# Token rows in float32 for the experts' gathers, and two more slots in the weights' ring

## The chip, the cores and the metric

One core of one Trainium2 chip. The metric is the device time of one execution in microseconds (us). The kernel before took 3013.36 us (median of three runs, 3009.52 to 3018.86). A difference of about 0.3%, 9 us, is what a measurement of this kernel can tell from none.

## The reference

Two blocks of two layers each work on 512 tokens of width 1024. The change lies in the second block, in its mixture of experts, which both layers of that block have:

```python
def ec_moe(h, w_router, w_gate, w_up, w_down):      # h: (1, 512, 1024), 16 experts
    cap = max(1, EC_FACTOR * n // N_EXPERTS)        # 64 tokens for each expert
    aff = softmax(einsum('bnd,de->bne', h, w_router))
    gate, idx = top_k(swapaxes(aff, 1, 2), cap)
    xs = h[idx]                                     # every expert's own 64 tokens
    a = silu(einsum('becd,edf->becf', xs, w_gate)) * einsum('becd,edf->becf', xs, w_up)
    out = einsum('becf,efd->becd', a, w_down) * gate[..., None]
    return zeros.at[idx].add(out)
...
# second_block: layer 0 = even mixer, ec_moe; layer 1 = pool mixer (w_in_odd, w_pool_grp), ec_moe; then a norm
```

Each of w_gate, w_up and w_down is 16 x 1024 x 1024 float32 in either layer: 192 MB a layer.

## The kernel before, in words

The stages follow one another: the first block, the even mixer, the experts of layer 0 (`c0`), the odd mixer (`d`), the experts of layer 1 (`c1`), the final norm. x lies transposed on chip (8 slices k of 128 features by 512 tokens).

`moe` (L1912) does one layer of experts. Its head: the router's products, the softmax, the top-k on VectorE (DVE; eight rounds of `max` and `match_replace`, L1962 and L1963), then a mask `mk`, a running count `ps` and from both `ptk`, each token's place with each expert. Beside the top-k `tokens` writes the normed tokens as rows: PE (TensorE) transposes x, ScalarE (ACT) scales into `tf`, rounds `tf` to fp32r into `tH`, and GpSimd (POOL) subtracts to get the rest `tL`. `tH` and `tL` are two X tiles each; the tag X has four buffers of 2048 columns (`big`, L258).

Then come eight pairs of experts, q = 0 to 7. The products of pair q want 8 loads of w_exp_gate, 8 of w_exp_up and 8 of w_exp_down, 1 MB each; gate(q), up(q) and down(q) below name those loads or the products on them (`pm` for gate and up, `pa` for down). PE takes them two loads at a time, one expert on either half of the array's columns. The tokens of an expert are fetched by a product as well: `gather(k, q)` multiplies token rows (stationary, 128 x 128) with one-hots `oh` (128 x 256, for four experts), for each of the four token blocks once with `tH` and once with `tL`, and ACT writes `xs[k]`. A set of 8 gathers serves two pairs of experts. The set for q = 0 lies between the first products of gate(0), two gathers ahead of each pair of loads. The later sets follow the gates of q = 1, 3 and 5, where they alternate with `scatter`, the products that add a pair's output to x (one-hots `ohn`, outputs `yH` and `yL`). In the last pair, q = 7, down is done in halves of 512 columns. `evict` at q = 6 takes an X tile for its first output (`big`).

```python
        ring = self.rings[kind]
        i = self.turns[kind] = (self.turns[kind] + 1) % len(ring)
        pool, tag, bufs, width = ring[i]
        return pool.tile([128, width], F32, name=tag, tag=tag, bufs=bufs)
```

That is `slot` (L314). Each load asks `raw` (L321, its DMA is L328) for the next slot of a ring of tiles in turn; a slot is written again when the products on it are done. The ring has 14 slots in both layers. A DMA's name in the trace says which tag it went to (rawx, raw, split, ox). All weight loads are issued by SyncE (SP). The order of PE's instructions in the experts is the program's (`manual_schedule`, L2046); that of SP, ACT, DVE and POOL is set by the scheduler when the kernel is built, and an engine takes its instructions in that order, so that one which waits holds up those behind it. The buffers of a tag are handed out in the program's order of requests.

`begin` (L1795) is the start of the odd mixer, run in steps inside the tail of `c0`: it loads the first 256 columns of w_in_odd to a ring slot, splits them into two more slots, and multiplies them with x. The other columns of w_in_odd are loaded by stage `d` itself.

Of the kernel before, what the change touches and what calls it, by code (L numbers as in the profile page):

```python
# [9 lines left out]
F32 = mybir.dt.float32  # L10
F32R = mybir.dt.float32r
I32 = mybir.dt.int32
AF = mybir.ActivationFunctionType
OP = mybir.AluOpType
# [5 lines left out]
D = 1024  # L20
S = 512
KC = 8
# [146 lines left out]
class Net:  # L169
# [379 lines left out]
    def gain(self, norm, sc, name):  # L549
        A = self.g.tile([128, KC], F32, name=name)  # L550
        self.stt(A, sc, 1.0, norm, OP.add, OP.mult)
        return A
# [1242 lines left out]
    def begin(self, A, B, pool):  # L1795

        r = self.rings["raw"]
        self.rings["raw"], self.turns["raw"] = [r[11], r[13], r[7], r[8], r[9], r[10], r[12]], -1
        (w,) = self.raw(self.a["w_in_odd"].rearrange("(k p) n -> p k n", p=128)[:, :, 0:256])
        H, L = [self.slot("raw").bitcast(F32R)[:, 0:2048].rearrange("p (k n) -> p k n", n=256) for i in range(2)]  # L1800
        for k in range(0, KC, 4):
            self.split(w[:, k:k + 4], H[:, k:k + 4], L[:, k:k + 4], self.nc.gpsimd)
        yield
        X = self.hl()
        self.tight = True
        p = [self.psm()[:, 0:256] for b in range(4)]

        def product(k):
            for b in range(4):
                T = slice(b * 128, b * 128 + 128)  # L1810
                self.mm(p[b], X[0][k][:, T], H[:, k], k == 0, False)
                self.mm(p[b], X[0][k][:, T], L[:, k], False, False)
                self.mm(p[b], X[1][k][:, T], H[:, k], False, k == KC - 1)

        for k in range(KC):
            self.act(X[0][k], self.x[k], AF.Copy, scale=A[:, k:k + 1])
            self.stt(X[1][k], self.x[k], A[:, k:k + 1], X[0][k].bitcast(F32), OP.mult, OP.subtract)
            if k:
                product(k - 1)
            yield  # L1820
        product(KC - 1)
        kept, self.pg = self.pg, "pa"
        y = self.rstd(self.acc, self.acl, pool.tile([128, 4], F32, name="oy"))
        c = self.shifted(w, B)
        self.pg = kept
        u = pool.tile([128, 2048], F32, name="ox", tag="ox", bufs=1)[:, 0:1024].rearrange("p (b n) -> p b n", b=4)
        for b in range(4):
            self.stt(u[:, b], p[b], y[:, b:b + 1], c, OP.mult, OP.add)
        self.begun = X, u, y
# [82 lines left out]
    def moe(self, l, A, B, gt, begin=None):  # L1912
        nc, g, m = self.nc, self.nc.gpsimd, self.m
# [5 lines left out]
        y = self.rstd(self.acc, self.acl)  # L1919
        ls = self.t([128, 512], "ls")  # L1920
        self.act(ls, pr)
        p = self.psm()
# [13 lines left out]
        p = self.psm()  # L1936
# [1 line left out]
            self.tr(p[0:16, b * 128:b * 128 + 128], aff[:, b])  # L1938
        work, have = self.accs[0:16], p[0:16]

        tH = [self.big([128, 2, D], F32R) for i in range(2)]
        tL = [self.big([128, 2, D], F32R) for i in range(2)]
        def tokens(i, ready):
            for b in range(4):
                p = self.psd()
                for k in range(4):
                    tr = self.tr(p[:, k * 128:k * 128 + 128], self.x[i * 4 + k][:, b * 128:b * 128 + 128])
                    if i:
                        self.after(tr.ins, ready)
                o = slice(i * 512, i * 512 + 512)  # L1950
                f = self.t([128, 512], "tf")
                c = self.act(f, p, AF.Copy, scale=y[:, b:b + 1])
                if not i:
                    self.after(c.ins, ready)
                self.act(tH[b // 2][:, b % 2, o], f)
                self.tt(tL[b // 2][:, b % 2, o], f, tH[b // 2][:, b % 2, o].bitcast(F32), OP.subtract, g)

        tokens(0, exp)

        for r in range(8):  # L1960
            m8 = self.t([128, 8], "m8")[0:16]
            nc.vector.max(m8, have)  # L1962
            mr = nc.vector.match_replace(work, m8, have, -1.0)  # L1963
            have = work
            if r == 4:
                tokens(1, mr.ins)
# [4 lines left out]
        p, pt = self.psm(), self.t([128, 4, 16], "ptk")  # L1971
# [10 lines left out]
        def gather(k, q):  # L1982
            if k == 0:
                for b in range(4):
                    self.tt(oh[b], self.bcm(self.C("iota"), 4), self.bc(pt[:, b, 2 * q:2 * q + 4], 64), OP.is_equal)
            p = self.psd()[:, 0:256]
            for b in range(4):
                r = oh[b].rearrange("p e c -> p (e c)")
                o = slice(k // 2 * 256 + k % 2, k // 2 * 256 + 256, 2)
                self.mm(p, tH[b // 2][:, b % 2, o], r, b == 0, False)  # L1990
                self.mm(p, tL[b // 2][:, b % 2, o], r, False, b == 3)
            self.act(xs[k], p, AF.Identity, scale=ab[:, 0, k:k + 1], bias=ab[:, 1, k:k + 1])

        def gates(q):

            ohq = [oh[b][:, q % 2 * 2:q % 2 * 2 + 2].rearrange("p e c -> p (e c)").bitcast(F32) for b in range(4)]
            pg = self.psd()
            for b in range(4):
                self.mm(pg[:, 0:2], ohq[b], aff[:, b, 2 * q:2 * q + 2], b == 0, b == 3)
            gv = self.t([128, 1], "gv")  # L2000
            for i in range(2):
                nc.vector.tensor_copy(gv[64 * i:64 * i + 64], pg[64 * i:64 * i + 64, i:i + 1])
            p = self.psd()
            for b in range(4):
                self.tr(p[:, b * 128:b * 128 + 128], ohq[b])
            ohn = self.t([128, 512], "ohn", F32R)
            self.act(ohn, p)
            return gv, ohn
# [9 lines left out]
            self.resid(k, p, gt[:, k:k + 1])  # L2018

        def onehot():  # L2020
            return [self.t([128, 4, 64], "oh", F32R) for b in range(4)], [m.tile([128, 256], F32, name="xs", tag="xs", bufs=8) for k in range(KC)]

        def evict(p, gv, big=False):
            if big:
# [20 lines left out]

        with self.tc.manual_schedule(engines={mybir.EngineType.PE}):  # L2046
            oh, xs = onehot()
            back = None
            for q in range(8):
                xo = (q % 2) * 128  # L2050
                pp = [self.psm() for i in range(4)]
                for wi, W in enumerate((Wg, Wu)):
                    for k2 in range(4):
# [4 lines left out]
                        for kk in range(2):  # L2058
                            k = 2 * k2 + kk
# [12 lines left out]
                if more:  # L2072
                    oh, xs = onehot()
                aT = []
                for k in range(KC):
# [4 lines left out]
                    if k in (5, 7):  # L2080
                        p = self.psd()
                        for i in range(4):
                            o = i // 2 * 256 + i % 2
# [8 lines left out]
        py = [self.psm("pa") for i in range(2)]  # L2092

        down(7, aT, py, [(0, 512, 4), (512, 512, 4)], lambda: begin and next(begin))
        self.last = [4, 5, 6, 7]
        hl = []
        for k in range(KC):
            if k % 4 == 0:
                hl.append(evict(py[k // 4], gv))
            scatter(k, back, (ohn, hl))  # L2100
            self.sqacc(k)
            if begin:
                next(begin)
        if begin:
            self.run(begin)
# [16 lines left out]
def build(nc, tc, a, cwhere, pwhere):  # L2122
    with ExitStack() as ctx:
        n = Net(nc, tc, ctx, a, cwhere, pwhere)
        g = n.g
# [18 lines left out]
        for l in range(2):  # L2144
            with ExitStack() as st:
# [23 lines left out]
                X = n.norm_hl(None if u else gain(), col(mods[l], 0), u)  # L2169
# [35 lines left out]
            with ExitStack() as st:  # L2205
                n.open(st, f"f{l}", {"2": 30 - l, "B2": 4}, {"pd": 4, "pm": 4}, 3, 3)
                X = n.norm_hl(n.gain(n.P(f"norm_ffn{l}"), col(mods[l], 4), f"Af{l}"), col(mods[l], 3))
# [10 lines left out]
        with ExitStack() as st:  # L2218
# [6 lines left out]
            m = n.m  # L2225
# [6 lines left out]
            X = n.norm_hl(n.gain(n.P("g10"), col(mod2[0], 1), "Ae"), col(mod2[0], 0))  # L2232
# [6 lines left out]
        for l in range(2):  # L2239
            if l == 0:  # L2240
                odd = ctx.enter_context(ExitStack())
                od = odd.enter_context(tc.tile_pool(name="od", bufs=1, reuse_waits="tile"))
            else:
                with ExitStack() as st:
                    n.open(st, "d", {"0": 8, "1": 14, "2": 16}, {"pd": 2, "pm": 6}, 3, 4)
                    n.rings["raw"] = n.rings["raw"][2:] + n.rings["raw"][:1]
                    n.odd(col(mod2[1], 0), col(mod2[1], 2))
                odd.close()
            with ExitStack() as st:
                n.open(st, f"c{l}", {"0": 8, "1": 8, "2": 8}, {"pa": 2, "pd": 2, "pm": 4}, 9 + l, 0, 2048)  # L2250
                n.phase, n.behind = "c", n.loaded
                begin = None
                if l == 0:
                    own, gen = n.rings["raw"][:9], n.rings["raw"][9:]
                    n.rings["raw"] = own[:8] + [(od, "ox", 1, 2048)] + gen[2:] + gen[:2] + own[8:]
                    begin = n.begin(n.gain(n.P("g11"), col(mod2[1], 1), "Ao"), col(mod2[1], 0), od)
                n.moe(l, Ar[l], col(mod2[l], 3), col(mod2[l], 5), begin)
                if l == 1:
                    n.final()
# [43 lines left out]
```

## Time and profile before

| what | us |
|---|---|
| median of 3 runs | 3013.36 |
| profiled execution | 3024.81 |
| its span | 3022.8 |
| PE busy | 2814.5 (93%) |
| DVE busy | 1427.0 (47%) |
| ACT busy | 898.2 (30%) |
| POOL busy | 365.5 (12%) |
| experts of layer 0, first gather to the gates of q = 7 | 1954.36 to 2396.98 |
| experts of layer 1, first gather to the gates of q = 7 | 2536.19 to 2976.96 |

The profiled execution is 0.38% longer than the median; its instants are counted from the start of its span. A busy share is an average over stages with different limits. A row of a timeline gives the start, the length from the first to the last instruction of a run of like ones, engine, line, operation, output and inputs, shape, count, and in brackets how long the engine stood before it and for whom. A float32 matmul shows as two records in the trace, one of fp32r as one. The granted clock (PEclk) is the share of TensorE's full 2.4 GHz.

### The profile page before, as it was taken

How to read it: one execution, taken by the hardware profiler on the slowest of the kernel's cores; microseconds unless marked ns; L12 is line 12 of the kernel's file. 1: busy time of each engine (PE TensorE's matmuls, PEld its weight loads, DVE VectorE, ACT ScalarE, POOL GpSimd, SP SyncE). 2: the span in 40 equal slices, each digit the busy share in tenths (PEclk: the TensorE clock that was granted, in tenths of full speed). 3: DMA queues.
4: the chain of work that ended last, by engine and by line, in shares of the span. 5: the costliest groups of instructions: out<-in, count | busy, mean ns of one | idle time of the engine just before them, and what ended most of it. 6: DMA issues, size and time to landing. Idle time of an engine off the chain costs nothing.

```text
span 3022.8 us, 42266 instructions
## 1 busy us (share of the span) xinstructions
PE 2814.5 (93%) x17407; PEld 1928.2 (64%) x17407; DVE 1427.0 (47%) x2686; ACT 898.2 (30%) x1720; POOL 365.5 (12%) x286
## 2 busy tenths in 40 slices
PE   7998999999999799999999979899899988999897
PEld 5876578888887657888899965534334375434333
DVE  4455565565546758779743675502111163111112
ACT  4323433223433344423343545311101123101101
POOL 0131112011023202212200220100000021000000
PEclk9997899999999699999999989899999998999999
DMA  6223155565220016489721100599999927999996
GB/s 225 70 71 124 36 160 163 182 182 164 84 75 26 2 41 200 135 267 315 244 59 56 50 22 14 215 408 420 420 420 421 394 82 305 421 421 421 421 421 273
DMA packets 287553, 636.98 MB, mean 211 GB/s; under 512 B 16896, under 2 KB 204544, under 8 KB 240256
## 3 DMA queue, kind: packets, MB, share of 16 engines
q1 hardware_dynamic: 285280, 634.15, 56.5%
q8 instruction: 137, 2.24, 0.3%
q10 hardware_dynamic: 2080, 0.13, 0.0%
q14 instruction: 56, 0.46, 0.0%
HBM read 632.14 MB, written 2.10 MB: 210 GB/s over the span
## 4 chain that ended last, share of the span: by engine, by line
PE 70%; DMA 16%; DVE 10%; ACT 2%; issue 1%; SPq 0%; POOL 0%; DVEq 0%; ACTq 0%; POOLq 0%
PE pd L297 40%; PE pm L297 9%; DMA rawx<-w_exp_up 5%; DMA rawx<-w_exp_gate 4%; PE pa L297 4%; PE pg L297 4%; PE pe L297 3%; PE po L297 3%; PE ph L297 3%; DMA rawx<-w_exp_down 2%; PE pd L301 2%; DMA split<-w_exp_up 1%; DVE aacc L294 1%; PE pn L297 1%; DMA raw<-ada_w 1%
## 5 line engine op out<-in xcount | busy, mean ns | idle before, releaser
L297 PE MATMUL pd<-X,split 128*128 128x512 f32 x2640 | 630.8, 394 | 11.7 <-ACT X L274 7.2
L297 PEld LDWEIGHTS pd<-X,split 128*128 128x128 f32 x2640 | 494.2, 189 | 121.6 <-ACT X L274 9.8
L297 PE MATMUL pm<-rawx,xs 128*64 128x512 f32 x1400 | 334.9, 595 | 30.1 <-DMA rawx<-w_exp_up 21.3
L297 PEld LDWEIGHTS pm<-rawx,xs 128*64 128x64 f32 x1400 | 108.3, 137 | 231.3 <-issue 169.5
L285 DVE TENSOR_TENSOR ms<-ms,pm 128x512 f32<-128x512 f32 x32 | 22.0, 688 | 485.9 <-PE pm L297 485.9
L274 ACT ACTIVATE split<-raw 128x1024 fp32r<-128x1024 f32 (+5 forms) x165 | 142.5, 869 | 204.2 <-PE pd L297 132.4
L285 DVE TENSOR_TENSOR split<-raw,split 128x1024 fp32r<-128x1024 f32 (+4 forms) x136 | 150.7, 1113 | 88.0 <-ACT split L274 87.1
L297 PE MATMUL pd<-split,X 128*128 128x256 f32 x1296 | 178.8, 292 | 9.6 <-ACT split L274 6.2
L297 PEld LDWEIGHTS pd<-split,X 128*128 128x128 f32 x1296 | 164.5, 195 | 16.3 <-ACT split L274 6.4
L297 PE MATMUL pd<-X,splitx 128*128 128x512 f32 x720 | 173.8, 391 | 0.0
L297 PE MATMUL pa<-rawx,maT 128*64 128x512 f32 x704 | 165.6, 595 | 0.1
L297 PEld LDWEIGHTS pd<-X,splitx 128*128 128x128 f32 x720 | 135.3, 188 | 29.8 <-DVE splitx L285 0.6
L297 PE MATMUL pd<-aH,split 128*128 128x512 f32 x484 | 153.2, 389 | 0.0
L294 DVE SCALAR_TENSOR_TENSOR aacc<-rawx,cs_c,aacc 128x512 f32<-128x512 f32 x160 | 133.8, 878 | 0.0
L294 DVE SCALAR_TENSOR_TENSOR x<-pd,modl,x 128x512 f32<-128x512 f32 x120 | 89.1, 750 | 76.6 <-PE pd L297 75.3
L294 DVE SCALAR_TENSOR_TENSOR yL<-pa,gv,yH 128x512 fp32r<-128x512 f32 x30 | 22.5, 750 | 205.6 <-ACT yH L274 203.8
L285 POOL TENSOR_TENSOR aL<-sg,aH 128x512 fp32r<-128x512 f32 x44 | 66.0, 1501 | 385.5 <-ACT aH L274 385.5
L297 PEld LDWEIGHTS pa<-rawx,maT 128*64 128x64 f32 x704 | 51.7, 137 | 91.6 <-issue 89.4
L297 PE MATMUL pm<-split,xs 128*64 128x512 f32 x288 | 98.7, 594 | 8.0 <-DMA split<-w_exp_up 5.3
L297 PEld LDWEIGHTS pd<-aH,split 128*128 128x128 f32 x484 | 90.8, 188 | 19.5
L274 ACT ACTIVATE split<-rawx 128x1024 fp32r<-128x1024 f32 (+3 forms) x63 | 59.0, 940 | 147.9 <-PE pd L297 119.8
L297 PE MATMUL pm<-raw,xs 128*64 128x512 f32 x288 | 97.3, 594 | 5.8 <-DMA raw<-w_exp_up 5.3
(692 smaller groups left out, 4621.2 us busy)
## 6 DMA issues: line engine op xcount, KB each, us to landing
rawx<-w_exp_gate SPq DMA_DIRECT2D x92, 1024.0 KB, 19.8
rawx<-w_exp_up SPq DMA_DIRECT2D x83, 1024.0 KB, 18.4
rawx<-w_exp_down SPq DMA_DIRECT2D x76, 1024.0 KB, 19.8
rawx<-w_mod SPq DMA_DIRECT2D x29, 1024.0 KB, 5.5
raw<-ada_w SPq DMA_DIRECT2D x27, 1024.0 KB, 5.2
raw<-w_in SPq DMA_DIRECT2D x22, 1024.0 KB, 5.1
raw<-w_exp_up SPq DMA_DIRECT2D x20, 1024.0 KB, 19.5
split<-w_exp_up SPq DMA_DIRECT2D x20, 1024.0 KB, 19.8
```

The costliest lines, as they stand in the source:

```text
L274: i = self.nc.scalar.activation(out, in_, f, **k)
L285: return (eng or self.nc.vector).tensor_tensor(out, a, b, op)
L294: return self.nc.vector.scalar_tensor_tensor(out, a, s, b, op0, op1)
L297: return self.nc.tensor.matmul(out, l, r, start=start, stop=stop, skip_group_check=True)
L301: return self.nc.tensor.transpose(out, x, self.C("ident")[0:k, 0:k])
```

## The change

The token rows are held once, as float32, in two X tiles instead of four; rounding and subtract go, ACT writes the tile itself, and a gather is four float32 matmuls instead of eight of fp32r. The one-hots become float32. Two slots of tag X join the ring, which has 16 slots now; in layer 0 they stand behind the nine own slots, in layer 1 at the end. `begin` takes other slots of the ring.

```diff
 def begin(self, A, B, pool):
-        self.rings["raw"], self.turns["raw"] = [r[11], r[13], r[7], r[8], r[9], r[10], r[12]], -1
+        self.rings["raw"], self.turns["raw"] = [r[0], r[1], r[2], r[12], r[13], r[14], r[15]], -1
...
 def moe(self, l, A, B, gt, begin=None):
-        tH = [self.big([128, 2, D], F32R) for i in range(2)]
-        tL = [self.big([128, 2, D], F32R) for i in range(2)]
+        tok = [self.big([128, 2, D]) for i in range(2)]
...
-                f = self.t([128, 512], "tf")
-                c = self.act(f, p, AF.Copy, scale=y[:, b:b + 1])
+                f = self.act(tok[b // 2][:, b % 2, o], p, AF.Copy, scale=y[:, b:b + 1])
                 if not i:
-                    self.after(c.ins, ready)
-                self.act(tH[b // 2][:, b % 2, o], f)
-                self.tt(tL[b // 2][:, b % 2, o], f, tH[b // 2][:, b % 2, o].bitcast(F32), OP.subtract, g)
+                    self.after(f.ins, ready)
...
-                self.mm(p, tH[b // 2][:, b % 2, o], r, b == 0, False)
-                self.mm(p, tL[b // 2][:, b % 2, o], r, False, b == 3)
+                self.mm(p, tok[b // 2][:, b % 2, o], r, b == 0, b == 3)
...
-            return [self.t([128, 4, 64], "oh", F32R) for b in range(4)], [m.tile([128, 256], F32, name="xs", tag="xs", bufs=8) for k in range(KC)]
+            return [self.t([128, 4, 64], "oh") for b in range(4)], [m.tile([128, 256], F32, name="xs", tag="xs", bufs=8) for k in range(KC)]
...
 def build(nc, tc, a, cwhere, pwhere):
+                own, gen = n.rings["raw"][:9 + l], n.rings["raw"][9 + l:]
+                X2 = [(n.xp, "X", 4, 2048)] * 2
+                n.rings["raw"] = own + gen + X2
                 if l == 0:
-                    own, gen = n.rings["raw"][:9], n.rings["raw"][9:]
-                    n.rings["raw"] = own[:8] + [(od, "ox", 1, 2048)] + gen[2:] + gen[:2] + own[8:]
+                    n.rings["raw"] = own + X2 + gen[1:2] + [(od, "ox", 1, 2048)] + gen[2:] + gen[:1]
```

SP, layer 0, before: the loads of gate(7), of up(7) and the first of down(7) (halves of 512 columns), then the first other columns of w_in_odd (an "x2" is a run of two).

```order
292 L328 DMA rawx<-w_exp_gate 128x2048 x8
293 L328 DMA ox<-w_exp_up 128x2048
294 L328 DMA split<-w_exp_up 128x2048 x2
295 L328 DMA raw<-w_exp_up 128x2048 x2
296 L328 DMA rawx<-w_exp_up 128x2048 x3
297 L328 DMA rawx<-w_exp_down 128x2x512 x8
298 L328 DMA ox<-w_exp_down 128x2x512 x2
299 L328 DMA split<-w_exp_down 128x2x512 x3
300 L328 DMA raw<-w_in_odd 128x8x256
```

The same place of SP in the change:

```order
295 L328 DMA rawx<-w_exp_gate 128x2048
296 L328 DMA raw<-w_exp_gate 128x2048
297 L328 DMA ox<-w_exp_gate 128x2048
298 L328 DMA split<-w_exp_gate 128x2048 x2
299 L328 DMA raw<-w_exp_gate 128x2048
300 L328 DMA rawx<-w_exp_up 128x2048 x6
301 L328 DMA X<-w_exp_gate 128x2048 x2
302 L328 DMA rawx<-w_exp_up 128x2048 x2
303 L328 DMA X<-w_exp_down 128x2x512 x2
```

Six loads of gate(7) come in their place; the two that go to X slots come behind six of up(7), whose own slots are those of down(6).

PE in the change, the same place: the end of down(6) (`pa`) and the first products of gate(7) (`pm`), 8 matmuls for each pair of loads.

```order
2525 L297 MATMUL pa<-rawx,maT 64x512 x32
2526 L297 MATMUL pm<-rawx,xs 64x512
2527 L297 MATMUL pm<-X,xs 64x512
2528 L297 MATMUL pm<-rawx,xs 64x512
2529 L297 MATMUL pm<-X,xs 64x512
2530 L297 MATMUL pm<-rawx,xs 64x512
2531 L297 MATMUL pm<-X,xs 64x512
2532 L297 MATMUL pm<-rawx,xs 64x512
2533 L297 MATMUL pm<-X,xs 64x512 x2
2534 L297 MATMUL pm<-raw,xs 64x512
```

The first X load is wanted in the first pair of gate(7), the second in the second pair. Before, these rows read `pm<-rawx,xs` throughout.

SP in the change, layer 1, the same loads:

```order
368 L328 DMA rawx<-w_exp_gate 128x2048 x2
369 L328 DMA raw<-w_exp_gate 128x2048 x2
370 L328 DMA split<-w_exp_gate 128x2048 x2
371 L328 DMA rawx<-w_exp_up 128x2048 x6
372 L328 DMA X<-w_exp_gate 128x2048 x2
373 L328 DMA rawx<-w_exp_up 128x2048 x2
374 L328 DMA X<-w_exp_down 128x2x512 x2
```

Here too the X loads of gate(7) come behind six of up(7). PE wants both in the fourth pair of gate(7), its last.

## Rows read from the trace of the kernel before

**Rows 1.** The page: GB/s in 40 slices, and one group of DMA issues.

```profile
GB/s 225 70 71 124 36 160 163 182 182 164 84 75 26 2 41 200 135 267 315 244 59 56 50 22 14 215 408 420 420 420 421 394 82 305 421 421 421 421 421 273
...
rawx<-w_exp_gate SPq DMA_DIRECT2D x92, 1024.0 KB, 19.8
```

**Rows 2.** PE's waits, layer 0's experts (1950 to 2460): total, times, longest.

```profile
PE pm L297 <- DMA rawx<-w_exp_up: 10.6, 8, 1.3
...
PE pm L297 <- DMA rawx<-w_exp_gate: 4.6, 5, 1.3
```

**Rows 3.** Busy time by stretch: PE, PEld, DVE, ACT, POOL, PEclk, DMA share, GB/s.

```profile
2245.00:2305.00 60.00, 50.76 (x254) 23.72 (x250) 7.69 (x12) 7.34 (x13) 0.00 (x0) 1.00 1.01 420
2305.00:2345.00 40.00, 39.63 (x179) 15.22 (x175) 7.69 (x12) 3.77 (x6) 0.00 (x0) 1.00 1.01 419
2345.00:2400.00 55.00, 47.78 (x218) 17.34 (x218) 4.60 (x8) 5.64 (x8) 0.00 (x0) 1.00 1.02 414
```

**Rows 4.** Timeline of SP, the ring's first filling in layer 0.

```profile
1932.77 0.33 SPq L328 DMA_DIRECT2D split<-w_exp_up  x1
1962.35 0.80 SPq L328 DMA_DIRECT2D rawx<-w_exp_up  x2
```

**Rows 5.** Busy time by stretch, the start of both layers' experts.

```profile
1936.00:1952.00 16.00, 7.58 (x32) 5.62 (x32) 12.96 (x30) 10.72 (x18) 9.83 (x8) 0.50 1.01 417
...
1954.00:1958.00 4.00, 3.64 (x16) 3.49 (x16) 2.56 (x8) 0.57 (x1) 0.00 (x0) 0.50 0.00 0
1958.00:1962.00 4.00, 4.00 (x17) 1.24 (x16) 0.00 (x0) 0.56 (x1) 0.00 (x0) 0.83 0.00 0
...
2542.00:2544.00 2.00, 2.00 (x13) 0.90 (x10) 0.00 (x0) 0.00 (x0) 0.00 (x0) 1.00 0.00 0
```

**Rows 6.** Timeline of POOL, the rests of the token rows in layer 0.

```profile
1939.49 9.83 POOL L285 TENSOR_TENSOR X<-tf,X 128x512 fp32r<-128x512 f32 x8 [43.88 <-ACT X L274]
```

**Rows 7.** Timeline of PE, the first gathers and products of layer 0.

```profile
1951.45 0.61 PE L301 MATMUL pm<-cst_g,mk 16*128 16x16 f32 x4 [6.33 <-DVE mk L290]
...
1954.36 3.75 PE L297 MATMUL pd<-oh,X 128*128 128x256 f32 x16 [0.93 <-DVE oh L285]
1958.05 4.27 PE L297 MATMUL pm<-rawx,xs 128*64 128x512 f32 x16
1962.25 2.20 PE L297 MATMUL pd<-oh,X 128*128 128x256 f32 x16
1964.38 3.65 PE L297 MATMUL pm<-rawx,xs 128*64 128x512 f32 x16
```

**Rows 8.** Timeline of PE, a float32 matmul on the whole array (two records).

```profile
130.24 1.02 PE L297 MATMUL pg<-dg,cst_a 128*128 128x512 f32 x2
```

**Rows 9.** Timeline of PE, end of layer 0's experts and the odd mixer.

```profile
2346.48 3.65 PE L297 MATMUL pa<-rawx,maT 128*64 128x512 f32 x16
...
2360.27 7.89 PE L297 MATMUL pm<-rawx,xs 128*64 128x512 f32 x34
...
2396.98 1.05 PE L297 MATMUL pd<-aff,oh 128*128 128x2 f32 x8
...
2448.12 0.79 PE L297 MATMUL pd<-split,X 128*128 128x256 f32 x2 [6.24 <-ACT split L274]
```

**Rows 10.** Timeline of SP, the last pair of layer 0 and the odd mixer.

```profile
2336.14 17.73 SPq L328 DMA_DIRECT2D rawx<-w_exp_gate  x8
2356.03 0.33 SPq L328 DMA_DIRECT2D ox<-w_exp_up  x1
...
2441.79 0.37 SPq L328 DMA_DIRECT2D rawx<-w_in_odd  x1
```

**Rows 11.** Timeline of PE, the last pair of layer 1.

```profile
2940.33 7.89 PE L297 MATMUL pm<-rawx,xs 128*64 128x512 f32 x34
...
2953.46 3.65 PE L297 MATMUL pm<-rawx,xs 128*64 128x512 f32 x16 [1.31 <-DMA rawx<-w_exp_gate]
...
2976.96 1.05 PE L297 MATMUL pd<-aff,oh 128*128 128x2 f32 x8
```

More of the change, by code (lines that the diff above doesn't have):

```diff
@@ L1989, in gather @@
                 o = slice(k // 2 * 256 + k % 2, k // 2 * 256 + 256, 2)
-                self.mm(p, tH[b // 2][:, b % 2, o], r, b == 0, False)
-                self.mm(p, tL[b // 2][:, b % 2, o], r, False, b == 3)
+                self.mm(p, tok[b // 2][:, b % 2, o], r, b == 0, b == 3)
             self.act(xs[k], p, AF.Identity, scale=ab[:, 0, k:k + 1], bias=ab[:, 1, k:k + 1])
         def gates(q):
-            ohq = [oh[b][:, q % 2 * 2:q % 2 * 2 + 2].rearrange("p e c -> p (e c)").bitcast(F32) for b in range(4)]
+            ohq = [oh[b][:, q % 2 * 2:q % 2 * 2 + 2].rearrange("p e c -> p (e c)") for b in range(4)]
             pg = self.psd()
```

## The prediction

> **What bounds the kernel now.** The page comes first, for where the core's DMA engines are full: the line of GB/s has two plateaus at 420 [rows 1], the two mixture-of-experts stages. Each moves 192 loads of 1 MB. At 420 GB/s a load takes 2.49 us, and 8 are outstanding, since one lands 19.8 us after its issue (8 x 2.49 = 19.9) [rows 1]. Next, the waits of PE (TensorE) in layer 0: they name weight loads, in pieces of at most 1.3 us, about 22 us in all with the smaller lines [rows 2]; layer 1 reads alike. The stretches show how this is spread: PE is busy 50.76 of 60 us in 2245 to 2305 and 39.63 of 40 in 2305 to 2345, while DMA stays at 420 in both [rows 3]. So the loads set the pace; PE falls behind in an even pair q (experts 2q and 2q+1) and catches up in the next. Only two things shorten such a stage: loads that begin earlier, and no pause in the queue. The pause in sight is at the start. SP issues the 14th load at 1932.77, the ring is full, and the next goes out at 1962.35, when the first products give back slots [rows 4]. DMA carries nothing from about 1952 to 1962, and in layer 1 from 2540 to 2544 [rows 5].
>
> **The change, part by part.**
>
> *Token rows.* Eight roundings on ACT and eight subtracts on POOL go in each layer. POOL's end at 1949.3 [rows 6]; PE's next step waits for DVE's mask of the top-k, and PE starts it at 1951.45 [rows 7]. That cover hides all sixteen, so I take 0; without it at most the subtracts' last 1.2 us would count.
>
> *Gathers.* Per slice k, 8 rounded matmuls become 4 in float32. Now a pair of slices takes 2.13 us (1962.25 to 1964.38) [rows 7], 0.133 per matmul. The new shape isn't in the trace. A float32 matmul appears there as two records. Lower bound: 0.27, as much as the two that it replaces. Upper: 0.51, half of the 1.02 that one of 512 columns took [rows 8]. The expert products, float32 too, take 3.45 per pair of loads (down(6), four pairs, 2346.48 to 2360.27) [rows 9], which is 16 records of 512 columns, eight on either half of the array: 0.43 a record, so for half the columns 0.215 a record and 0.43 a matmul. I take that, the commonest row: 3.4 a pair, **1.3 more**, some 5 us for a set of 8 slices, four sets a layer. The three sets behind q = 1, 3 and 5 lie where PE is the later one by 5 to 10 us and then catches up in 7 to 8 us of waits [rows 2, 3]: 0 on the path, while the queue has loads. If it has not, 5 us each.
>
> The Trainium skill's "FP8 and Floating Point Precision" (TensorE Precision Notes) counts float32 as four passes. Four at the 0.133 of a rounded matmul make 0.53, an estimate; by it the sum would be some 6 us larger.
>
> *Two more slots at the start.* Loads 15 and 16 go out before the pause: 2 x 2.49 = 5.0 us less, if the queue then keeps up. But its next slots come from products behind slower gathers. The first pair of gathers runs at half the granted clock until about 1959 [rows 5, 7], so it takes some 6.0 instead of 3.7; the first products then end at 1963.8 instead of 1962.25 (+1.5, half made good by the clock being up), the next three at 1.3 more each: +5.4 at the fourth. Loads 23 and 24 then leave at 1984.8 and have landed at 1989.8; today it is 1989.4. **Net 0 in each layer** (between -5 and +3): the two slots buy what the gathers cost.
>
> *The last pair of experts, layer 0.* This decides. The orders show that SP issues the two loads of w_exp_gate that go to X slots behind six of w_exp_up; those six wait for down(6) to free the ring's first slots. PE's program wants the first X load in its first pair of products of gate(7). The first load of gate(7) lands at 2356.0, where the next issue shows a lane free [rows 10]; the X load is thirteenth: 2356.0 + 12 x 2.49 = 2385.9. PE is done with down(6) at 2360.27 today [rows 9], 5.4 later with one set of gathers still to make good: 2365.7. It then stands 20 us. Behind that nothing waits any more: eight pairs x 3.45 = 27.6, so up(7) ends at 2413.5, today 2396.98 [rows 9]. **+16.5.**
>
> *Layer 1.* Here the X loads are pair four of gate(7). Today that pair's loads have landed at 2953.46 and the end of up(7) is 2976.96 [rows 11]. Six of gate(7) land by 2948.4, six of up(7) by 2963.4, then X at 2965.9 and 2968.4. PE has done three pairs at 2951.9 and stands until 2968.4; five pairs x 3.45 give 2985.7. **+8.7.**
>
> *Clock.* After such a stand the granted clock should fall, as when PE idles in the top-k (0.50, the lower of its two levels, 1.2 GHz) [rows 5]. The first work after it lost 1.5 us in the gathers and 0.6 in the products [rows 7]: **+2 per layer**, between 0 and 3.
>
> *Into the odd mixer.* Today the third load of w_in_odd leaves SP at 2441.79 [rows 10], when PE's last product of `begin` frees its slot, and PE waits 6.24 for its split [rows 9]. Now this load goes to a slot that down(7) frees earlier. Gain 0 to 8; I take **-4**, since ACT's splits stand in line behind it.
>
> Sum: 16.5 + 8.7 + 4 - 4 = **+25**. The profiled execution took 3024.81, 0.38% over the median of 3013.36, so it would go to 3050 and the median to **3038**.
>
> **Rivals.**
>
> *Room is what was missing (faster).* The place is the pause at each start. The price is 5.0 per layer and 4 to 8 at the odd mixer: 3013 - 15 = 2998. It decides by where the late X loads land: within 4 us of their issue near 2362, so before PE wants them. That needs a queue nearly empty then; DMA at 420 in that stretch [rows 3] speaks against it.
>
> The Trainium skill's "Perfetto Trace Analysis" (Optimization Strategy) says that the same gap repeated on the engine that should be saturated can mean too little SBUF for the next tile. PE's 1.3 us gaps look so, and by that rule the two slots would also take away up to 22 us a layer (some 2970). The trace disagrees: the loads run at 420 GB/s through every such gap.
>
> *It cancels (same).* The slots gain 3 a layer, the X loads cost only half since DMA is late by then and PE too: 6 to 12 saved in layer 0's stand, nothing lost at the clock: 3013 + 5.
>
> *Gathers dearer (slower still).* At 0.51 a pair takes 4.1, so 2 more than today: load 24 lands 3 later in each layer and the sets behind q = 1 and 3 leave PE later than the waits give back, 3 more: 3038 + 12 = 3050.
>
> *Only one of the two stands comes (slower, less).* If the queue serves the X loads of one layer early: 3013 + 10 to 17, say 3026. The extreme is a change that does nothing: an X slot that is never filled early. The orders exclude it, with X loads ahead of the first products in both layers.
>
> **How the numbers follow.** A measurement of this kernel tells 0.3%, 9 us, from nothing. Forecast 0.60 (3028 to 3046 by its own bounds), dearer gathers 0.14, one stand 0.10: all slower, 0.84. Cancelling 0.10, faster 0.06. The range reaches down into the cancelling case and up over the dearer gathers: 3014 to 3054, leaving out the faster case, some of the cancelling one and the far end above.
>
> **What would show it.** Right: in layer 0 a PE wait of 15 to 22 us for X<-w_exp_gate near 2365 to 2386, in layer 1 one of 11 to 17 near 2952 to 2968; gathers of 3.4 us a pair where the clock is full; the pause at the start shorter by some 3 us, with a second small one behind it; all else in the MoE stages in place. Wrong: no wait for X above 5 us, which would kill the largest term; gathers near 2.2 or 4.3 a pair; an odd mixer that starts no earlier relative to the end of down(7); or a start where load 24 lands 5 us earlier than now, in which case 5 us a layer come off the sum.

## The result, and the profile after

The change takes 3045.01 us (median of 6 runs) against 3016.11 us of the kernel before beside it (6 runs): ratio 1.0079, 95% interval 1.0057 to 1.0101. That is 17 to 30 us more by the interval; the forecast was 25 more, 3038 us. The profiled execution took 3044.46 us.

Executions of these kernels differ by up to 22 us in the stages ahead of the experts (the first gather of layer 0 starts at 1938 to 1961 us). There the kernels differ only in the token rows, in the ring that the first loads go to and, in e7, in the added matmuls; from the first `max` of the top-k to the first gather it is 15.3 to 15.4 us in each of them. So traces are compared from that first gather on. The table gives stretches between PE rows of the timelines: the first `pd<-oh,X` of a layer, its last `pd<-aff,oh` (the gates of q = 7), and the end of the span. There is one trace for each kernel; e4 has the experts of the kernel before, and its two layers agree with those of before within 0.4 us.

| kernel | layer 0, first gather to gates of q = 7 | to first gather of layer 1 | layer 1, first gather to gates of q = 7 | to the end | sum |
|---|---|---|---|---|---|
| before | 442.6 | 139.2 | 440.8 | 45.8 | 1068.4 |
| the change | 463.5 | 131.4 | 453.4 | 46.3 | 1094.6 |
| e1 | 450.4 | 138.7 | 448.7 | 46.4 | 1084.2 |
| e2 | 449.7 | 139.1 | 448.2 | 46.2 | 1083.2 |
| e3 | 442.5 | 138.3 | 442.0 | 45.7 | 1068.5 |
| e4 | 442.7 | 142.5 | 441.1 | 46.1 | 1072.4 |
| e5 | 443.6 | 138.1 | 443.9 | 47.1 | 1072.6 |
| e6 | 438.0 | 138.1 | 436.5 | 46.0 | 1058.6 |
| e7 | 444.9 | 137.9 | 442.8 | 45.8 | 1071.3 |

The change: +20.9 in layer 0, +12.6 in layer 1, -7.8 between them, +26.2 in all.

The page of the change, GB/s in 40 slices (before: [rows 1]):

```profile
GB/s 223 70 73 121 35 163 160 183 188 164 76 70 26 2 59 208 140 291 316 181 73 56 42 21 15 306 407 418 420 420 420 316 61 336 417 421 421 421 421 215
```

The two plateaus stand at 420 as before, so the loss lies in few places. PE's waits in layer 0's experts (1950 to 2480), to be read beside [rows 2]:

```profile
PE pm L297 <- DMA X<-w_exp_gate: 19.7, 1, 19.7
PE pd L297 <- ACT xs L274: 4.1, 21, 0.2
...
PE pm L297 <- DMA rawx<-w_exp_up: 1.8, 2, 1.3
```

The 1.3 us pieces are nearly gone, and one wait for an X load is nearly as long as all of them were. SP around it:

```profile
2350.18 8.72 SPq L328 DMA_DIRECT2D rawx<-w_exp_up  x6
2361.01 2.82 SPq L328 DMA_DIRECT2D X<-w_exp_gate  x2
...
2400.51 0.39 SPq L328 DMA_DIRECT2D rawx<-w_in_odd  x1
```

PE at the same place, the first X product and the gates of q = 7 (before: [rows 9]):

```profile
2354.71 5.75 PE L297 MATMUL pa<-rawx,maT 128*64 128x512 f32 x26
2360.29 1.02 PE L297 MATMUL pm<-rawx,xs 128*64 128x512 f32 x2
...
2380.97 1.12 PE L297 MATMUL pm<-X,xs 128*64 128x512 f32 x1 [19.67 <-DMA X<-w_exp_gate]
...
2411.15 1.05 PE L297 MATMUL pd<-aff,oh 128*128 128x2 f32 x8
```

The load was issued at 2361.01 and is waited for until 2380.97: 20 us, the 8 loads that are outstanding at once. Such a long wait of PE is called a stand below. Layer 1, PE (before: [rows 11]):

```profile
2974.89 1.97 PE L297 MATMUL pm<-X,xs 128*64 128x512 f32 x2 [10.32 <-DMA X<-w_exp_gate]
2977.38 4.55 PE L297 MATMUL pm<-X,xs 128*64 128x512 f32 x13 [0.51 <-DMA X<-w_exp_gate]
...
2996.02 1.05 PE L297 MATMUL pd<-aff,oh 128*128 128x2 f32 x8
```

The start of layer 0 in the change, PE (before: [rows 7]):

```profile
1947.69 6.16 PE L297 MATMUL pd<-oh,X 128*128 128x256 f32 x16 [0.93 <-DVE oh L285]
1953.78 3.65 PE L297 MATMUL pm<-rawx,xs 128*64 128x512 f32 x16
1957.36 3.73 PE L297 MATMUL pd<-oh,X 128*128 128x256 f32 x16
1961.02 3.65 PE L297 MATMUL pm<-rawx,xs 128*64 128x512 f32 x16
```

The first pair of gathers takes 6.1 us, each later one 3.66 (1957.36 to 1961.02), before 2.13. POOL's subtracts [rows 6] have no row any more. SP there (before: [rows 4]):

```profile
1929.16 4.01 SPq L328 DMA_DIRECT2D X<-w_exp_up  x2
1957.45 22.53 SPq L328 DMA_DIRECT2D rawx<-w_exp_down  x8
```

The two X loads go out ahead of the pause; the eight behind it then take 22.5 us to issue, waiting for slots. Busy time by stretch of the kernel before, from 8 us ahead of its first gather to 40 us behind it:

```profile
1946.36:1954.36 8.00, 1.18 (x8) 1.02 (x9) 6.72 (x15) 0.74 (x2) 2.97 (x3) 0.50 0.71 296
1954.36:1994.36 40.00, 40.00 (x203) 19.71 (x204) 3.72 (x10) 5.72 (x10) 0.00 (x0) 0.94 0.75 299
```

The same of the change:

```profile
1939.69:1947.69 8.00, 1.19 (x9) 1.03 (x9) 6.86 (x15) 0.22 (x1) 0.00 (x0) 0.50 1.01 422
1947.69:1987.69 40.00, 40.00 (x170) 21.24 (x172) 2.20 (x7) 5.70 (x10) 0.00 (x0) 0.94 0.67 260
```

Counted as time missing at 421 GB/s, before lacks 8 x (1 - 296/421) + 40 x (1 - 299/421) = 14.0 us, the change 40 x (1 - 260/421) = 15.3: 1.3 later, though two loads went early.

### The profile page after: what moved, and what is told of

The parts are those of the page before. It is cut to its first block, busy times and chain, and to the rows that moved or that the text cites. A ratio compares the mean times of both kernels' runs of the same rounds, so it can differ in the third digit from the quotient of the medians.

```text
span 3042.3 us, 42206 instructions
## 1 busy us (share of the span) xinstructions
PE 2845.5 (94%) x17407; PEld 1957.8 (64%) x17407; DVE 1426.2 (47%) x2686; ACT 889.0 (29%) x1704; POOL 344.8 (11%) x270
## 4 chain that ended last, share of the span: by engine, by line
PE 74%; DMA 12%; DVE 10%; ACT 3%; issue 1%; POOL 0%; SPq 0%; DVEq 0%; ACTq 0%; POOLq 0%
PE pd L297 41%; PE pm L297 12%; PE pa L297 5%; PE pg L297 4%; PE pe L297 3%; PE po L297 3%; DMA rawx<-w_exp_down 3%; PE ph L297 3%; DMA split<-w_exp_gate 2%; PE pd L301 2%; DMA rawx<-w_exp_up 1%; DMA X<-w_exp_gate 1%; DVE aacc L294 1%; PE pn L297 1%; DMA raw<-ada_w 1%
## 5 line engine op out<-in xcount | busy, mean ns | idle before, releaser
L297 PE MATMUL pm<-rawx,xs 128*64 128x512 f32 x1216 | 287.2, 595 | 3.2 <-DMA rawx<-w_exp_up 3.1
L297 PEld LDWEIGHTS pm<-rawx,xs 128*64 128x64 f32 x1216 | 92.0, 137 | 184.6 <-issue 173.3
L297 PE MATMUL pa<-rawx,maT 128*64 128x512 f32 x608 | 140.8, 594 | 0.1
L297 PE MATMUL pd<-oh,X 128*128 128x256 f32 x512 | 129.9, 401 | 9.2 <-ACT xs L274 6.8
L297 PEld LDWEIGHTS pd<-oh,X 128*128 128x128 f32 x512 | 99.0, 202 | 43.0 <-ACT xs L274 22.5
L297 PE MATMUL pm<-X,xs 128*64 128x512 f32 x256 | 90.1, 619 | 30.5 <-DMA X<-w_exp_gate 30.5
L294 DVE SCALAR_TENSOR_TENSOR yL<-pa,gv,yH 128x512 fp32r<-128x512 f32 x30 | 22.5, 751 | 197.1 <-ACT yH L274 195.3
## 6 DMA issues: line engine op xcount, KB each, us to landing
rawx<-w_exp_gate SPq DMA_DIRECT2D x76, 1024.0 KB, 19.9
```

Of the source, the lines that this page charges most:

```text
L294: return self.nc.vector.scalar_tensor_tensor(out, a, s, b, op0, op1)
L297: return self.nc.tensor.matmul(out, l, r, start=start, stop=stop, skip_group_check=True)
```

## The experiments

**e1: no X tile for an output.**

```diff
-                    back = ohn, [evict(py[n], gv, q == 6 and n == 0) for n in range(2)]
+                    back = ohn, [evict(py[n], gv) for n in range(2)]
```

> The changed kernel with one edit: the outputs of the pair q = 6 both go to ordinary tiles, none to an X tile, so that no request for an X tile stands between the ring's X loads of q = 6 and those of q = 7. The order then shows SP issuing the two X loads of gate(7) before the loads of gate(7) that go to other slots. Theory (the late X loads cost the time): both stands of PE, 19.7 us in layer 0 and 10.8 us in layer 1, are gone, with them some 2 us each at the lower clock; about 30 us less than the change, so about 0.2% under the kernel before (the odd mixer's start still 8 us earlier): ratio to before 0.996 to 1.000. Rival (the slower gathers have made the loads late, and the stands only show it): the stands turn up as waits for other loads, and the ratio stays at 1.004 to 1.008.

Ratio 1.0066 (1.0039 to 1.0093). The stands are gone, but only 13 and 5 us with them, and the time looks like the rival's. SP shows that the edit changed more than it was meant to:

```profile
2290.79 3.34 SPq L328 DMA_DIRECT2D X<-w_exp_gate  x2
2294.22 0.38 SPq L328 DMA_DIRECT2D raw<-w_exp_up  x1
...
2329.66 5.51 SPq L328 DMA_DIRECT2D X<-w_exp_down  x3
...
2350.17 15.49 SPq L328 DMA_DIRECT2D rawx<-w_exp_up  x8
```

With nothing between the requests, SP issues X loads too early: two of gate(7) ahead of most of up(6), four halves of down(7) ahead of all of up(7). Either is 2 MB, 5 us of the queue, before what PE wants next, and in layer 0's q = 7 PE waits six times 1.1 to 1.4 us (e5, below, has two such waits). So e1 has another order of loads that differs from that of their use, and does not decide between theory and rival.

**e2: the ring of before.** Only the float32 gathers are left of the change.

```diff
-        self.rings["raw"], self.turns["raw"] = [r[0], r[1], r[2], r[12], r[13], r[14], r[15]], -1
+        self.rings["raw"], self.turns["raw"] = [r[11], r[13], r[7], r[8], r[9], r[10], r[12]], -1
...
-                own, gen = n.rings["raw"][:9 + l], n.rings["raw"][9 + l:]
-                X2 = [(n.xp, "X", 4, 2048)] * 2
-                n.rings["raw"] = own + gen + X2
                 if l == 0:
-                    n.rings["raw"] = own + X2 + gen[1:2] + [(od, "ox", 1, 2048)] + gen[2:] + gen[:1]
+                    own, gen = n.rings["raw"][:9], n.rings["raw"][9:]
+                    n.rings["raw"] = own[:8] + [(od, "ox", 1, 2048)] + gen[2:] + gen[:2] + own[8:]
```

> The changed kernel with the ring of before (14 slots, no X slot) and the order of slots that the odd mixer's beginning had before; only the float32 gathers are left. Theory: no X load, so no stand at q = 7; the two slots' 5 us at the start are missing and the slower gathers delay the release of slots, so 5 us more per layer with the sets in the middle hidden: ratio to before 1.002 to 1.005, with PE's first gathers at 3.4 to 3.7 us a pair and the pause of the loads at the start 2 us longer than before. Rival (the gathers are the cost): 1.007 or more, the whole loss of the change.

Ratio 1.0076 (1.0047 to 1.0105), by the stretches +14.8 us, 0.5%: no stand, +7.1 and +7.4 in the layers where 5 each were expected. The interval reaches from the theory's upper end to the rival's, and by its ratio alone e2 is no faster than the change (1.0079), so the verdict rests on the trace. Its start:

```profile
1931.09:1939.09 8.00, 1.18 (x8) 1.03 (x9) 6.86 (x15) 0.22 (x1) 0.00 (x0) 0.50 0.74 307
1939.09:1979.09 40.00, 40.00 (x168) 21.19 (x170) 2.20 (x7) 5.71 (x10) 0.00 (x0) 0.93 0.60 228
```

Missing of full transfers: 2.2 + 18.3 = 20.5 us, 6.5 more than before, where 2 was expected. The slower gathers hold the slots back, and without the two slots that is paid in full.

**e3: gathers of the rounded part, on e1.** (Token rows and one-hots of fp32r, one matmul for each token block; the rests are left out.)

```diff
-        tok = [self.big([128, 2, D]) for i in range(2)]
+        tok = [self.big([128, 2, D], F32R) for i in range(2)]
...
-            return [self.t([128, 4, 64], "oh") for b in range(4)], [m.tile([128, 256], F32, name="xs", tag="xs", bufs=8) for k in range(KC)]
+            return [self.t([128, 4, 64], "oh", F32R) for b in range(4)], [m.tile([128, 256], F32, name="xs", tag="xs", bufs=8) for k in range(KC)]
...
```

> The kernel of e1 whose gathers read the rounded part of the token rows alone (four fp32r matmuls a slice; the rests are left out, so the experts see rounded tokens). Theory: this takes away the price of the gathers and leaves the two slots; a pair of gathers takes 1.1 us instead of 3.4 to 3.7, the first slots come back 2 us earlier than before the change and the loads do not pause again, so the two slots' 5 us are kept: 5 to 8 us per layer less than e1, ratio to before 0.991 to 0.995. Rival (the first gathers cost nothing since the loads set the pace anyway): within 3 us of e1.

Ratio 1.0007 (0.9989 to 1.0025): the forecast for it failed against the kernel before, though it took 8 and 7 us off e1. It was up 5.7 us at the gates of q = 5 (317.4 against 323.1 from the first gather) and lost them in q = 6 and 7, where e1 has its other order of the X loads.

**e4: the kernel before with other slots for the odd mixer's beginning.**

```diff
-        self.rings["raw"], self.turns["raw"] = [r[11], r[13], r[7], r[8], r[9], r[10], r[12]], -1
+        self.rings["raw"], self.turns["raw"] = [r[0], r[1], r[13], r[8], r[9], r[10], r[12]], -1
```

> The kernel before with one edit: the beginning of the odd mixer takes the ring's own slots 0, 1 and 13 for its weights and their split instead of 11, 13 and 7, as the change does in its ring. The order then shows the third load of w_in_odd no longer behind the products of that beginning. Theory: PE's wait of 6.2 us for the split of these columns goes, and the time from the gates of q = 7 to the first gather of layer 1 falls from 139 us to 131 to 133: ratio to before 0.997 to 0.999. Rival (that gain in the change comes from the later end of the experts, behind which more is already loaded): no wait goes, ratio 1.000.

Ratio 1.002 (1.0002 to 1.0037). The expected gain did not come, and the wait stays. PE in e4:

```profile
2449.45 2.12 PE L297 MATMUL pm<-rawx,X 128*128 128x256 f32 x16
2458.00 0.79 PE L297 MATMUL pd<-split,X 128*128 128x256 f32 x2 [6.43 <-ACT split L274]
```

and SP issues the load at 2451.63, right behind those products, so these slots alone don't free its place; the stretch between the layers is 3.3 us longer.

**e5: the X slots at places 6 and 7 of the ring**, where the last pair's X loads are the last of up(7).

```diff
-                n.rings["raw"] = own + gen + X2
+                n.rings["raw"] = own[:6] + X2 + own[6:] + gen
...
-                    n.rings["raw"] = own + X2 + gen[1:2] + [(od, "ox", 1, 2048)] + gen[2:] + gen[:1]
+                    n.rings["raw"] = own[:6] + X2 + own[6:] + gen[1:2] + [(od, "ox", 1, 2048)] + gen[2:] + gen[:1]
```

> The changed kernel with the two X slots moved to places 6 and 7 of the ring. In the last pair they then fall to the last two loads of up(7), behind six others that wait for down(6) anyway, and the order shows every load of q = 7 in PE's order; the one exception left is in q = 6, where two loads of down(6) go ahead of up(6). Float32 gathers, 16 slots and the X output of q = 6 stay. Theory (late X loads cost what is left of the loss, slots and gathers cancel): no stand at q = 7; from the first gather to the gates of q = 7 some 443 to 446 us in layer 0 and 441 to 444 in layer 1 (before 442.6 and 440.8, the change 463.5 and 453.4), ratio to before 0.997 to 1.001. Rival (after e1: the float32 gathers cost 15 us that the two slots do not give back): 450 and 448 as in e1 and e2, ratio 1.004 to 1.007.

Ratio 1.0017 (0.9999 to 1.0035); 443.6 and 443.9 us where 443 to 446 and 441 to 444 were expected and the rival had 450 and 448. SP's order and PE's waits in layer 0 (1943 to 2460):

```profile
2342.61 12.78 SPq L328 DMA_DIRECT2D rawx<-w_exp_up  x6
2357.55 2.88 SPq L328 DMA_DIRECT2D X<-w_exp_up  x2
```

```profile
PE pd L297 <- ACT xs L274: 4.1, 21, 0.2
PE pm L297 <- DMA X<-w_exp_up: 2.7, 2, 1.4
...
PE pm L297 <- DMA rawx<-w_exp_up: 1.9, 3, 1.3
```

Same gathers, same 16 slots, another place of two of them: 22.0 us less than the change (1094.6 to 1072.6), and the interval of the ratio lies wholly below that of the change (1.0057 to 1.0101). This is the experiment that settles the cause: the late X loads cost 22 of the 26 us, and all else comes to the other 4.

**e6: e5 with e3's gathers.**

> The kernel of e5 with gathers of the rounded part alone (four fp32r matmuls a slice; the rests are left out, so the experts see rounded tokens). Theory: what is missing of full transfers at the start falls by 8 us as in e3, and the loads of q = 7 are now in order: 434 to 439 us to the gates of q = 7 in either layer, ratio to before 0.993 to 0.997. Rival (e3 gained nothing because the weights' pace allows no more than the kernel before has): 442 and ratio 1.000.

Ratio 0.9964 (0.9946 to 0.9983), 438.0 and 436.5 us: faster than both kernels, inside what was expected. Its start lacks less:

```profile
1939.63:1947.63 8.00, 1.18 (x8) 1.02 (x9) 6.86 (x15) 0.22 (x1) 0.00 (x0) 0.50 1.01 422
1947.63:1987.63 40.00, 39.45 (x186) 17.17 (x188) 3.89 (x11) 7.24 (x13) 0.00 (x0) 0.94 0.85 338
```

40 x (1 - 338/421) = 7.9 us, 6.1 under before. So the slots do pay where the gathers don't take it back; but e6's gathers are half of those of before as well, so its gain is not that of the slots alone.

**e7: e5 with idle matmuls ahead of the first gathers.**

```diff
...
+        def warm(n, w):
+            d = self.psd()
+            for i in range(n):
+                j = self.mm(d[:, 0:w], self.C("ident"), self.x[0][:, 0:w])
+                self.after(j.ins, self.turned)
+                self.turned = j.ins
+        warm(5, 512)
...
+            warm(1, 256)
...
```

> The kernel of e5 with seven float32 matmuls more in each layer that compute nothing used: five of 512 columns while PE waits for the top-k, one of 256 behind each group of small transposes. Theory (the first pair of gathers takes 6 us instead of 3.7 because the granted clock is at its lower level): it starts at the higher one, the first slots come back 2.3 us earlier, the loads pause that much less, 2 us less per layer than e5. Rival (the clock does not rise from this, or the added matmuls hold up the transposes of the mask): first pair still 6 us, or the first gather later by 1 us, no difference to e5 or 2 us more.

Ratio 1.0024 (1.0005 to 1.0043), by the stretches 1.3 us under e5: no difference. The first pair still takes 6.1 us:

```profile
1941.53 4.56 PE L297 MATMUL pd<-x,cst_g 128*128 128x512 f32 x10
1949.71 0.42 PE L301 MATMUL pm<-cst_g,mk 16*128 16x16 f32 x4 [3.62 <-DVE mk L290]
...
1952.57 6.16 PE L297 MATMUL pd<-oh,X 128*128 128x256 f32 x16
```

The five matmuls ran at the full clock and were done 3.62 us ahead of PE's next work; in this form the rival holds. Matmuls that end later were not tried.

## Why the prediction was right, step by step

*The X loads of the last pair: right.* Layer 0's stand was to be 20 us, it was 19.67. The eight pairs of products behind it take 30.2 us (2380.97 to 2411.15) where 27.6 and 2 for the clock were put down. From the first gather on, the gates of q = 7 are 20.9 later, forecast 16.5 + 2. In layer 1 the stand was forecast at 16.5 us (11 to 17 as a sign) and was 10.8: the text let PE be done with three pairs at 2951.9, about where the kernel before is, though by its own 5.4 us later (2940.33 + 5.4 + 3 x 3.45) it is 2956. The slip does not touch the sum, since the landing of the second X load sets what follows (434.8 us behind the first gather, forecast 432.2). The gates are 12.6 later, forecast 8.7 + 2. e5 shows the mechanism: with these loads elsewhere both stands vanish.

*The start: right in kind, its parts a little off.* "Net 0 in each layer" came out as 1.3 us more of missing transfer in layer 0; e5, with no late load, ends its layers 1.0 and 3.1 us later than before. The first pause is some 3 us shorter, as put down (DMA carries next to nothing from about 1952 to 1963 before and from 1951 to 1958 in the change), and a second, small one lies near 1964. A pair of gathers takes 3.66 us, not 3.4, so the term "1.3 more" is 1.5 more; 0.46 us a matmul, between the bounds 0.27 and 0.51. Two slots were to be worth 5.0 a layer: e2 against e5, 14 slots against 16 with the same gathers, gives 6.1 and 4.3. The gathers were to take the same: e2 against before gives 7.1 and 7.4.

The Trainium skill's count of four passes ("FP8 and Floating Point Precision", TensorE Precision Notes) would have made 0.53 us, an estimate from four rounded matmuls of 0.133; the trace has 0.46. By its rule the gathers would have been dearer than they are.

*The gathers in the middle: right.* From the first gather on, the change is 12.3 later than before at the gates of q = 2, 3.3 at q = 3, 8.9 at q = 4, 1.3 at q = 5 and 6.7 at q = 6: each set puts PE back and the former waits give it back. PE waits 1.8 us for loads in layer 0 now, apart from the stand.

The Trainium skill's rule on repeated gaps ("Perfetto Trace Analysis", Optimization Strategy), that they can mean too little SBUF for the next tile, is not borne out here. The gaps of 1.3 us did go in the change, and no time with them: they were PE's slack at a pace that the loads set at 420 GB/s. Nor do they follow the count of slots: PE's waits for loads in layer 0 make 22 us before with 14 slots, 8 in e2 with 14 and slower gathers, and 24 in e6 with 16 and faster ones.

*Into the odd mixer: right in sign, in the wrong place.* Forecast -4, measured -7.8. But e5 has its third load of w_in_odd early too (25.8 us behind the gates; 17.5 in the change, 44.8 before) and gains 1.1, though PE's wait of 6.2 us there is 1.4 in e5. So 6.6 us come with the late X loads. What gives them back is argued: while PE stood, DMA went on with down(7), whose last load leaves SP 11.5 us ahead of the gates in the change and 7.8 us behind them in e5, and PE takes the products of down(7) in one stretch of 14.0 us in the change, in pieces over 22.4 us in e5. But the products of down(7) lie behind `manual_schedule`, so PE's order there is the scheduler's and differs between the two; what the loads and what the order gives was not separated. The late X loads thus cost 19.9 + 9.5 in the layers (against e5) and give 6.6 back between them, 22.8 (22.0 by the sums, with 0.8 less at the end). The term -4 was mis-sized: it is about -1, and the rest of the gain belongs to the first term.

*Token rows: nothing, as forecast.* PE waits for DVE's mask as before ([rows 7]: 6.33 us; now 8.27), and from the first `max` of the top-k to layer 0's first gather it is 15.3 us, before 15.4.

The sum of the forecast was +25, the stretches give +26.2. That it came so close is in part luck: the two layers cost 4.3 more than the 29.2 put down for them, and the stretch between them gave 3.8 more than its 4. What made the forecast right was reading where the scheduler had put two loads in SP's order; from the diff alone, 16 slots in place of 14, the same arithmetic says no change, which is what e5 measures within its interval.

What stays open: why those two loads were put there. That the X output of q = 6 is requested between two X loads is shown to matter (e1 changes the order); how the scheduler weighs it was not tried. The exact gathers with 16 slots and no late load (e5) are not faster than before; e6 is, and does less work.

## What to carry to other kernels

A queue that is issued in one order is part of the dependences: when a ring gains slots of a tag that others request too, look at where the new loads land in that order against the order of their use, at the end of the loop above all. Slots buy a stage that is bound by transfers only the loads that go out ahead of its start, here 2 x 2.5 us a layer (6.1 and 4.3 measured), and whatever lengthens the time to the first release is paid from the same purse. Work on an engine with slack costs nothing until the slack's last piece is gone, so count the slack by stage.

## What was not expected of the hardware

The clock in e7. Busy time by stretch, PEclk third from the end:

```profile
1941.50:1946.00 4.50, 4.47 (x10) 1.82 (x10) 4.29 (x10) 0.65 (x1) 0.00 (x0) 1.00 1.02 426
1946.00:1949.70 3.70, 0.09 (x1) 0.00 (x0) 3.50 (x9) 0.00 (x0) 0.00 (x0) 1.00 1.00 418
1949.70:1952.50 2.80, 2.50 (x12) 1.62 (x12) 1.93 (x4) 0.22 (x1) 0.00 (x0) 0.69 1.01 421
1952.50:1957.00 4.50, 4.50 (x12) 3.58 (x12) 2.26 (x7) 0.56 (x1) 0.00 (x0) 0.50 0.67 279
```

The granted clock stayed at its full level while PE stood idle after the added matmuls (0.09 of 3.70 us busy), and fell to the lower one, 1.2 GHz, when PE was at work again (2.50 of 2.80 us, then all the time). In the long stand of the change it fell while PE stood, and the first products behind it ran at the lower level:

```profile
2362.00:2380.00 18.00, 0.00 (x0) 0.00 (x0) 0.00 (x1) 0.00 (x0) 0.00 (x0) 0.60 1.01 420
2380.00:2384.00 4.00, 3.03 (x8) 1.01 (x10) 0.00 (x0) 0.00 (x0) 0.00 (x0) 0.50 1.01 420
```

So in both a stand is paid for by the work behind it, also where the clock was still full at its end, and the burst of matmuls that ended ahead of e7's stand did not help.
